# Values of the dilated attention stored from SBUF in three token orders, in place of copies from DRAM to DRAM

## The chip, the cores and the metric

The kernel runs on one core of a Trainium2 chip. The metric is the device time of one execution in microseconds (us); the median of three runs stands for a kernel. A core has five engines that run their own instruction streams in order: PE (matrix multiply), DVE (vector), ACT (scalar functions and copies), POOL, and SP, which here only issues DMAs. ACT issues DMAs too. Instructions wait for each other by semaphores.

## The reference

One decoder layer on 2048 tokens of width 1024, in float32: RMSNorm, one input projection, two attention mixers side by side, gates, and an output projection that is added to the input. Only the first mixer matters here. Its eight heads (64 wide) attend in three patterns at once, with strides 1, 4 and 16 between keys:

```
DILATED_PATTERNS = ((128, 1), (512, 4), (2048, 16))
proj = jnp.matmul(rmsnorm(x, norm_gain), w_in)
q_a, k_a, v_a, z_a, c_q, c_kv, k_rope, z_b = jnp.split(proj, idx, axis=-1)
v_a = v_a.reshape(B, S, A_HEADS, A_HEAD_DIM)
for window, dilation in DILATED_PATTERNS:
    o, m, den = dilated_pattern(q, k, v, rel_bias, window, dilation)
o_a = sum(alpha[..., None] * o)      # alpha: softmax over the three log denominators
mixed = concat([o_a * silu(z_a), o_b * silu(z_b)])
y = x + mixed @ w_out
```

In each pattern a token looks at the keys of its own residue class, so the values `v_a` are wanted by the kernel in three orders of tokens: as they are, grouped by residue modulo 4, and grouped by residue modulo 16.

## The kernel before

The first stage, up to some 705 us, is the input projection. It runs in two halves of eight token blocks (128 tokens each). In each half groups of columns follow each other: `g0 g1 q0 z0 q1 z1 k0 z2 k1 g2 z3` in half 0, `g0 g1 q0 q1 k0 k1 g2 z0 z1 z2 z3` in half 1 (lines 235 to 242). Per block, `mm_tok` (line 393) does 24 matmuls into one of three PSUM tiles, split in a high and a low part of both operands. The z groups (gates) multiply the other way round (`unit_z`, line 537) and keep their result in the DRAM tensors `GD`, through a tile `zst` of two buffers.

The values are in three of these groups: 64 columns in g0, 128 in g1, 320 in g2. `v_hi` (line 402) has ACT copy them from PSUM to the tile `vst`, which has two buffers; `v_lo` (line 407) stores them in the DRAM tensor `vA`, rows in the kernel's own order: within a block of 128 tokens the row is (residue modulo 16, then the eight tokens of that residue). `store` (line 180) puts a DMA off by one clock of the unit loop, `flush` (line 183) issues it from ACT. So there are 48 stores, one for each block and group.

`v_turn(n)` (line 411) then makes the other two orders for a quarter of the tokens, each by one copy of 1 MB from DRAM to DRAM issued from SP: `vA2` (order of stride 4, line 415) and `vA3` (order of stride 16, line 417). Quarters 0 and 1 are turned in the group q0 of half 1 (line 755), quarters 2 and 3 after the first loads of head 0 (lines 1265, 1266). These are places in the source: the first stage is not ordered by hand, a planner places the instructions on each engine's queue by its own estimates, and in the profile the copies stand at 310, 332, 567 and 588 us. From the second stage on, the order is written out by hand.

SP's queue in the first stage also carries the loads of the weights (`w_load`, line 246, into `wraw`, two buffers, freed by the splits of `w_split` on ACT, or POOL, and DVE, lines 271 to 274), of the input (`x_load`, line 194, three buffers `xt`), rows of the position bias (line 384) and, at its end, bias, Q and K of head 0 (`a_loadb`, `a_loadq`, `a_loadk`, lines 834, 814, 818). `h0`, `h1`, `h2` (lines 201 to 226) normalise a block of the input, transpose it on PE and split it into `hTh` and `hTl`.

The values are read in the second stage: `a_loadv(h, w)` (line 848) loads one head's columns of `vA`, `vA2` or `vA3`.

Of the kernel before, what the change touches and what calls it, by code (L numbers as in the profile page):

```python
# [101 lines left out]
def hybrid_kernel(ctx: ExitStack, tc: tile.TileContext, x, positions, rel_bias, norm_gain, w_in,  # L102
# [3 lines left out]
    pe, dve, act, pool, sp = nc.tensor, nc.vector, nc.scalar, nc.gpsimd, nc.sync  # L106
# [19 lines left out]
    vA = dr.tile([S, 512], F32, name="vA")  # L126
    vA2 = dr.tile([S, 512], F32, name="vA2")
    vA3 = dr.tile([S, 512], F32, name="vA3")
# [48 lines left out]
    deferred = []  # L177
    ends = []

    def store(dst, src):  # L180
        deferred.append((clock[0] + 1, dst, src))

    def flush(always=False):
        while deferred and (always or deferred[0][0] <= clock[0]):
            _, dst, src = deferred.pop(0)
            act.dma_start(dst, src)

    clock = [0]

# [4 lines left out]
    def x_load(b):  # L194
        XT[b] = xtile([128, D])
        sp.dma_start(XT[b], xv[b])
# [4 lines left out]
    def h0(b):  # L201
        st = P1.tile([128, 4], F32, name="hst", bufs=3)
        for u in range(2):
            act.activation(junk_tile(), XT[b][:, 512 * u:512 * u + 512], AF.Square, accum_out=st[:, 2 * u:2 * u + 1])
        dve.tensor_tensor(st[:, 1:2], st[:, 0:1], st[:, 2:3], op=OP.add)
        dve.tensor_scalar(st[:, 1:2], st[:, 1:2], 1.0 / D, EPS, op0=OP.mult, op1=OP.add)
        rstd_pow(st[:, 2:3], st[:, 1:2], 1)
        RST[b] = st
# [90 lines left out]
    for i, ap in enumerate((a_q_gain, a_k_gain, qn_gain, kn_gain)):  # L299
        src = bass.AP(tensor=ap.tensor, offset=ap.offset, ap=[[1, 64], [1, 1]])  # L300
# [104 lines left out]
        return v  # L405

    def v_lo(v, b, h0_):
        n = v.shape[1]
        store(vA[128 * b:128 * b + 128, 64 * h0_:64 * (h0_ + n)], v.rearrange("p h d -> p (h d)"))

    def v_turn(n):

        a, a2, a3 = vA[:], vA2[:], vA3[:]
        o = 512 * 512 * n
        sp.dma_start(bass.AP(tensor=a2.tensor, offset=a2.offset + o, ap=[[65536, 4], [4096, 16], [1, 4096]]),
                     bass.AP(tensor=a.tensor, offset=a.offset + o, ap=[[4096, 4], [16384, 16], [1, 4096]]))
        sp.dma_start(bass.AP(tensor=a3.tensor, offset=a3.offset + 16384 * n, ap=[[65536, 16], [4096, 4], [1, 4096]]),
                     bass.AP(tensor=a.tensor, offset=a.offset + o, ap=[[4096, 16], [65536, 4], [1, 4096]]))

    def qraw_tile():  # L420
        return P1.tile([128, 256], F32, name="qraw", bufs=5)
# [1 line left out]
    def unit_g0(key, b):  # L423
        st = {}

        def s1():
            ps = PS[key, b]
            m = st["m"] = P1.tile([128, 4], F32, name="cst", bufs=3)
            raw = st["raw"] = qraw_tile()
            act.activation(raw, ps[:, :256], AF.Copy)  # L430
            st["v"] = v_hi(1, ps[:, 256:320])
            act.activation(junk_tile()[:, :256], raw, AF.Square, accum_out=m[:, 0:1])

        def s2():
            m = st["m"]
            v_lo(st["v"], b, 0)
            dve.tensor_scalar(m[:, 1:2], m[:, 0:1], 1.0 / 256, EPS, op0=OP.mult, op1=OP.add)
            rstd_pow(m[:, 2:3], m[:, 1:2], 1)

        def s3():  # L440
            dve.tensor_scalar(st["raw"], st["raw"], st["m"][:, 2:3], None, op0=OP.mult)

        def s4():
            tp = tp_tile()
            for i in range(2):
                pe.transpose(tp[:, i, :], st["raw"][:, i * 128:(i + 1) * 128], ident)
            act.activation(cT[:, b % 8, 0:2, :], tp[:, 0:2, :], AF.Copy)

        return [lambda: mm_tok(key, 320, b), s1, s2, s3, s4]
# [39 lines left out]
    def unit_g2(key, b):  # L489
        st = {}  # L490

        def s1():
            st["v"] = v_hi(5, PS[key, b][:, :320])

        return [lambda: mm_tok(key, 320, b), s1, lambda: v_lo(st["v"], b, 3)]
# [41 lines left out]
    def unit_z(key, j, c, row):  # L537
        st = {}

        def s0():  # L540
            ps = st["ps"] = mm_tile() if P1 is not None else psZ.tile([128, 512], F32, name="mz", bufs=2)
            for k in range(8):
                mm3(ps, WH[key][:, k, j * 128:(j + 1) * 128], WL[key][:, k, j * 128:(j + 1) * 128],
                    hTh[c][:, k, :], hTl[c][:, k, :], k == 0, k == 7)

        def s1():
            t = PZ.tile([128, 512], F32, name="zst", bufs=ZST)
            act.activation(t, st["ps"], AF.Tanh, scale=0.5)
            dve.scalar_tensor_tensor(t, t, 1.0, st["ps"], op0=OP.add, op1=OP.mult)
            store(GD[row][:, c * 512:(c + 1) * 512], t)  # L550

        return [s0, s1]
# [128 lines left out]
    for gi, (half, nm) in enumerate(seq):  # L681
        key = (half, nm)
        units = []
        if nm[0] == "z":
            zi = int(nm[1])
            for c in (2 * half, 2 * half + 1):
                for j in range(2):
                    units.append(unit_z(key, j, c, 2 * zi + j))
        else:
            for b in range(8 * half, 8 * half + 8):  # L690
                if nm == "g0":
                    units.append(unit_g0(key, b))
                elif nm == "g1":
                    units.append(unit_g1(key, b))
                elif nm == "g2":
                    units.append(unit_g2(key, b))
                else:
                    units.append(unit_qk(key, b, 2 * int(nm[1]), nm[0] == "q"))
        nu = len(units)
        for i, unit in enumerate(units):  # L700
            if half == 1 and nm[0] == "z" and not (todo_bg or bg.live):
                late.append((gi, i, nu, unit))
                continue
            if nm == "g0" and half == 0:
                if i + 3 < 8:
                    x_load(i + 3)
                if i + 2 < 8:
                    h0(i + 2)
            if nm == "g0" and half == 1:
                b = 12 + i  # L710
                if i < 1:
                    x_load(b + 3)
                if i < 2:
                    h0(b + 2)
                if i < 4:
                    h1(b)
                    h2(b)
            clock[0] += 1
            flush()
            main.add(unit)  # L720
            main.tick()
            if nm == "g0" and half == 0 and i + 1 < 8:
                h1(i + 1)
                h2(i + 1)
            for u in (SPLIT8 if nu == 8 else SPLIT4)[i]:
                w_split(4 * gi + 4 + u)
            if half == 0 and gi == 9 and i == 5:
                for b in range(8, 11):
                    x_load(b)
            if half == 0 and gi == 9 and i in (6, 7):  # L730
                h0(2 + i)
            if half == 0 and gi == 10:
                if i == 0:
                    h0(10)
                    h1(8)
                if i == 1:
                    h1(9)
                if i == 2:
                    h2(8)
                    x_load(11)  # L740
                    h2(9)
                    x_load(12)
                    h1(10)
                    h0(11)
                if i == 3:
                    h2(10)
                    x_load(13)
                    h1(11)
                    h2(11)
                    x_load(14)  # L750
                    h0(12)
                    h0(13)
            if nm == "g0" and half == 0 and i == 5:
                rope_tables()
            if nm == "q0" and half == 1 and i in (0, 4):
                v_turn(i // 4)
            if nm == "g1":
                b = 8 * half + i
                todo_bg += [("q", b, clock[0]), ("k", b, clock[0] + 4)]
            credit = min(credit + RATE[half] * (1.5 if nm[0] == "z" else 1.0), 1.5)  # L760
            if credit >= 1 and todo_bg and todo_bg[0][2] <= clock[0]:
                credit -= 1
                kind, b, _ = todo_bg.pop(0)
                bg.add(post(b, kind))
            bg.tick()
            while ends:
                ends.pop(0)()
            if misc and not (nm == "g0" and half == 0):
                misc.pop(0)()
    main.drain()  # L770
    assert not ends
    while todo_bg:
        kind, b, _ = todo_bg.pop(0)
# [488 lines left out]
    a_loadq(0)  # L1262
    a_loadk(0, 0)
    a_loadk(0, 1)
    v_turn(2)
    v_turn(3)
    weave(zsteps[:ZC], seq_s(0))
    a_loadq(1)
    a_loadk(1, 0)
# [395 lines left out]
    for b in range(4, 16):  # L1665
        c, o = divmod(b, 4)
# [67 lines left out]
```

## Time and profile before

| | |
|---|---|
| median of three runs | 1694.55 us (1688.96 to 1695.15) |
| the profiled execution | 1694.15 us, span 1692.4 us |
| mean granted clock of TensorE in it | 0.983 |
| busy: PE, DVE, ACT, POOL | 1610.5, 963.2, 833.1, 670.7 us |
| DMA | 206.94 MB; read from HBM 139.60 MB, written 72.25 MB |

A profile is one execution. Its views name an instruction by line, engine, operation and tile; "idle before <-releaser" is the time in which its engine stood still before it, and what ended that. A wait in SP's or ACT's queue (SPq, ACTq) is that of the instruction that issues a DMA: it holds everything behind it on that engine. The granted clock is a share of 2.4 GHz.

### The profile page before, as it was taken

The numbers are of one execution on the slowest core, as the hardware profiler recorded it, in microseconds if no ns is written. First come the engines' busy times: TensorE is split into PE (matmuls) and PEld (weight loads), VectorE is DVE, ScalarE is ACT, GpSimd is POOL, SyncE is SP. The second block draws the span as 40 slices with busy tenths as digits, with TensorE's granted clock in tenths as the row PEclk, the third lists the DMA queues.
The fourth block names the chain that finished last, engine by engine and source line by source line (L and its number), as shares of the span: only waits on it lengthen the run. The fifth ranks groups of instructions, "written<-read, shape, count | busy, mean of one in ns | idle before, by whom it ended". The sixth has DMA issues, their size and how long they took to land. (4 is left out here: it accounts for less than half of the span.)

```text
span 1692.4 us, 29007 instructions
## 1 busy us (share of the span) xinstructions
PE 1610.5 (95%) x10028; PEld 1303.2 (77%) x10028; DVE 963.2 (57%) x2937; ACT 833.1 (49%) x2237; POOL 670.7 (40%) x699
## 2 busy tenths in 40 slices
PE   6999999989999979999999889999999999999998
PEld 5998899979999967888777566666666666567887
DVE  4655564254667215477778567767666666734331
ACT  5656454255666312458777755555555555530000
POOL 2364353014667101125565737754464361411000
PEclk8999999999999989999999999999999999999999
DMA  7357454551554683479985554312221221237652
GB/s 160 93 144 179 130 143 119 180 153 48 132 143 139 197 222 116 107 168 202 199 190 123 125 129 88 95 49 59 72 57 49 71 58 38 72 80 188 175 135 64
DMA packets 224711, 206.94 MB, mean 122 GB/s; under 512 B 102797, under 2 KB 189561, under 8 KB 218420
## 3 DMA queue, kind: packets, MB, share of 16 engines
q1 hardware_dynamic: 136852, 153.85, 36.3%
q10 hardware_dynamic: 87712, 51.24, 11.0%
q8 instruction: 79, 1.29, 0.3%
q14 instruction: 68, 0.56, 0.1%
HBM read 139.60 MB, written 72.25 MB: 125 GB/s over the span
## 5 line engine op out<-in xcount | busy, mean ns | idle before, releaser
L231 PE MATMUL mz<-wh,hTh 128*128 128x256 f32 (+2 forms) x600 | 182.9, 305 | 1.6 <-ACT hTh L225 1.6
L233 PE MATMUL mz<-wh,hTl 128*128 128x256 f32 (+2 forms) x600 | 179.0, 298 | 1.8 <-DVE hTl L226 1.8
L232 PE MATMUL mz<-wl,hTh 128*128 128x256 f32 (+2 forms) x600 | 178.1, 297 | 0.0
L1418 ACT ACTIVATE ptB<-T 128x512 f32<-128x512 f32 (+3 forms) x160 | 84.7, 529 | 169.2 <-PE T L1413 168.7
L1431 PE MATMUL O<-ptB,VB 128*64 128x512 f32 (+3 forms) x640 | 160.6, 559 | 2.0 <-DVE ptB L1416 2.0
L274 DVE SCALAR_TENSOR_TENSOR wl<-wraw,ng,wh 128x256 fp32r<-128x256 f32 (+2 forms) x176 | 83.1, 510 | 115.9 <-ACT wh L273 114.4
L1406 ACT ACTIVATE P<-P,msB 128x1024 f32<-128x1024 f32 (+4 forms) x104 | 109.4, 1052 | 65.5 <-DVE msB L1393 65.4
L1388 PE MATMUL S<-kBh,qBh 96*128 96x512 f32 (+2 forms) x320 | 133.4, 417 | 2.0 <-DVE msB L1393 2.0
L1388 PEld LDWEIGHTS S<-kBh,qBh 96*128 96x128 f32 x320 | 60.3, 189 | 94.0 <-issue 74.6
L231 PEld LDWEIGHTS mz<-wh,hTh 128*128 128x128 f32 x600 | 115.8, 193 | 3.8 <-ACT hTh L225 2.6
L233 PEld LDWEIGHTS mz<-wh,hTl 128*128 128x128 f32 x600 | 115.7, 193 | 2.6 <-DVE hTl L226 2.6
L1390 PE MATMUL S<-kBh,qBl 96*128 96x512 f32 (+2 forms) x320 | 116.7, 365 | 0.0
L1389 PE MATMUL S<-kBl,qBh 96*128 96x512 f32 (+2 forms) x320 | 116.5, 364 | 0.0
L232 PEld LDWEIGHTS mz<-wl,hTh 128*128 128x128 f32 x600 | 116.1, 193 | 0.1
L147 POOL TENSOR_TENSOR pst<-pst,CM 128x8 f32<-128x8 f32 x48 | 80.3, 1686 | 82.6 <-DVE pst L598 73.8
L273 ACT ACTIVATE wh<-wraw,ng 128x256 fp32r<-128x256 f32 (+2 forms) x168 | 76.5, 514 | 68.3 <-DMA wraw<-in_w_in_dram 40.2
L231 PE MATMUL po<-woh,mh 128*128 128x512 f32 x256 | 101.8, 398 | 2.7 <-ACT woh L1294 2.1
L1416 DVE COPY ptB<-T 128x512 f32<-128x512 f32 (+3 forms) x160 | 96.8, 605 | 12.3 <-PE T L1413 11.5
L1393 DVE CUSTOM_DVE_ANT_0 P<-S,zero 128x512 f32<-128x512 f32 (+1 forms) x96 | 65.1, 678 | 66.9 <-PE S L1390 65.2
L1413 PE MATMUL T<-CM,P 128*128 128x128 f32 x740 | 100.0, 276 | 2.5 <-DVE gA__12590 L1242 1.2
L232 PE MATMUL po<-wol,mh 128*128 128x512 f32 x256 | 100.4, 393 | 1.2 <-POOL wol L1295 1.2
L233 PE MATMUL po<-woh,ml 128*128 128x512 f32 x256 | 100.7, 394 | 0.0
(492 smaller groups left out, 4553.3 us busy)
## 6 DMA issues: line engine op xcount, KB each, us to landing
wraw<-in_w_in_dram SPq DMA_DIRECT2D x72, 256.0 KB
V<-vA SPq DMA_DIRECT2D x24, 512.0 KB
xt<-in_x_dram SPq DMA_DIRECT2D x16, 512.0 KB
GD<-zst ACTq DMA_DIRECT2D x32, 256.0 KB
vA<-vA SPq DMA_DIRECT2D x8, 1024.0 KB
Q<-qT SPq DMA_DIRECT2D x8, 1024.0 KB
KH<-kT SPq DMA_DIRECT2D x16, 512.0 KB
KL<-kT SPq DMA_DIRECT2D x16, 512.0 KB
```

Of the source, the lines that this page charges most:

```text
L231: pe.matmul(ps, lh, rh, start=first, stop=False)
L232: pe.matmul(ps, lh, rl, start=False, stop=False)
L233: pe.matmul(ps, ll, rh, start=False, stop=last)
L274: dve.scalar_tensor_tensor(WL[key][:, k, :w], r[:, j, :w], ng[:, k:k + 1], f32(wh), op0=OP.mult, op1=OP.subtract)
L1388: pe.matmul(ps[:, :nm], H["q", "h"][:, q], H["k", "h"][:, k], start=True, stop=False)
L1389: pe.matmul(ps[:, :nm], H["q", "h"][:, q], H["k", "l"][:, k], start=False, stop=False)
L1390: pe.matmul(ps[:, :nm], H["q", "l"][:, q], H["k", "h"][:, k], start=False, stop=True)
L1406: act.activation(t, t, AF.Exp, bias=b, scale=-1.0, accum_out=H["den", c][:, i, d:d + 1])
L1413: pe.transpose(tp[:, d, :], p_part(h, c, d, 128 * j, 128), ident)
L1416: dve.tensor_copy(pt[:, d0:, :], tp[:, d0:, :])
L1418: act.activation(pt[:, d0:, :], tp[:, d0:, :], AF.Copy)
L1431: pe.matmul(o[64 * e:64 * e + 64, d0:, :], V[:, j + e, :], pt[:, d0:, :], start=(j == 0), stop=(j == 4 * c + 2), skip_group_check=True)
```

## The change

`v_turn` and its eight copies are gone. `v_lo` stores each unit's values three times from `vst`: to `vA` from ACT as before, to `vA3` by one DMA from SP, and to `vA2` by four DMAs from SP, one for each 32 partitions, since the order of stride 4 splits a block into four places. `store` takes the issuing engine as an argument. So each of the 48 units has six DMAs in place of one (240 more, all on SP), of 128 rows or four times 32 rows of 256, 512 or 1280 bytes, and `vst` is free again when all six have landed.

```diff
-    def store(dst, src):
-        deferred.append((clock[0] + 1, dst, src))
+    def store(dst, src, eng=act):
+        deferred.append((clock[0] + 1, dst, src, eng))
 
     def flush(always=False):
         while deferred and (always or deferred[0][0] <= clock[0]):
-            _, dst, src = deferred.pop(0)
-            act.dma_start(dst, src)
+            _, dst, src, eng = deferred.pop(0)
+            eng.dma_start(dst, src)
...
     def v_lo(v, b, h0_):
+
         n = v.shape[1]
-        store(vA[128 * b:128 * b + 128, 64 * h0_:64 * (h0_ + n)], v.rearrange("p h d -> p (h d)"))
-
-    def v_turn(n):
-
-        a, a2, a3 = vA[:], vA2[:], vA3[:]
-        o = 512 * 512 * n
-        sp.dma_start(bass.AP(tensor=a2.tensor, offset=a2.offset + o, ap=[[65536, 4], [4096, 16], [1, 4096]]),
-                     bass.AP(tensor=a.tensor, offset=a.offset + o, ap=[[4096, 4], [16384, 16], [1, 4096]]))
-        sp.dma_start(bass.AP(tensor=a3.tensor, offset=a3.offset + 16384 * n, ap=[[65536, 16], [4096, 4], [1, 4096]]),
-                     bass.AP(tensor=a.tensor, offset=a.offset + o, ap=[[4096, 16], [65536, 4], [1, 4096]]))
+        cols = slice(64 * h0_, 64 * (h0_ + n))
+        v = v.rearrange("p h d -> p (h d)")
+        store(vA[128 * b:128 * b + 128, cols], v)
+        store(vA3[:].rearrange("(i m a) c -> m i a c", i=16, a=8)[b, :, :, cols], v, sp)
+        for x in range(4):
+            store(vA2[:].rearrange("(n j x a) c -> n x j a c", n=4, j=4, a=8)[b // 4, 4 * (b % 4) + x, :, :, cols],
+                  v[32 * x:32 * x + 32], sp)
...
-            if nm == "q0" and half == 1 and i in (0, 4):
-                v_turn(i // 4)
...
-    v_turn(2)
-    v_turn(3)
```

## Rows read from the trace of the kernel before

**Rows 1.** First part of the page: busy time and share of the span.

```profile
PE 1610.5 (95%) x10028; PEld 1303.2 (77%) x10028; DVE 963.2 (57%) x2937; ACT 833.1 (49%) x2237; POOL 670.7 (40%) x699
```

**Rows 2.** Busy time by stretch; columns: us, PE, PEld, DVE, ACT, POOL, clock, DMA, GB/s.

```profile
66.00:98.00 32.00, 32.00 (x222) 28.53 (x221) 16.98 (x57) 20.68 (x83) 19.55 (x44) 1.00 0.38 110
...
296.00:324.00 28.00, 28.00 (x188) 27.54 (x187) 3.38 (x8) 5.48 (x14) 1.00 (x1) 1.00 0.61 190
...
344.00:362.00 18.00, 11.04 (x58) 10.17 (x57) 7.93 (x17) 9.47 (x25) 1.02 (x2) 0.82 0.64 183
580.00:645.00 65.00, 50.37 (x214) 40.69 (x212) 16.83 (x59) 13.26 (x29) 3.90 (x7) 0.89 0.71 198
```

**Rows 3.** Timeline of PE, 340 to 362 and 580 to 645: instructions after a gap.

```profile
348.20 0.84 PE L222 MATMUL tp<-CM,xt 128*128 128x128 f32 x4 [3.65 <-DVE hTl L226]
359.44 1.09 PE L222 MATMUL tp<-CM,xt 128*128 128x128 f32 x4 [3.31 <-DVE hTl L226]
...
582.22 0.33 PE L634 MATMUL tp<-CM,krr 128*128 128x128 f32 x1 [1.77 <-ACT sg L641]
603.31 0.79 PE L231 MATMUL mz<-hTh,wh 128*128 128x512 f32 x1 [4.40 <-DVE zst L549]
...
617.33 0.59 PE L891 MATMUL S<-KH,Q 128*128 128x256 f32 x3 [2.96 <-DMA KH<-kT]
...
638.70 0.58 PE L891 MATMUL S<-KH,Q 128*128 128x256 f32 x1 [4.85 <-DVE m L903]
```

**Rows 4.** Stretches just after these gaps, same columns as rows 2.

```profile
348.00:350.00 2.00, 1.79 (x9) 1.61 (x10) 1.34 (x3) 0.30 (x1) 0.00 (x0) 0.64 0.90 243
350.00:352.00 2.00, 2.00 (x10) 2.00 (x9) 0.00 (x0) 0.00 (x0) 0.00 (x0) 0.51 0.71 206
...
360.00:362.00 2.00, 2.00 (x10) 1.96 (x9) 1.36 (x4) 1.71 (x7) 0.46 (x1) 0.50 0.92 278
...
603.00:606.00 3.00, 2.69 (x6) 2.15 (x7) 1.05 (x3) 0.91 (x2) 0.00 (x0) 0.50 0.49 154
606.00:609.00 3.00, 3.00 (x11) 2.38 (x10) 0.77 (x2) 0.60 (x1) 1.20 (x2) 0.67 0.91 339
618.00:621.00 3.00, 3.00 (x9) 2.37 (x8) 0.00 (x0) 0.00 (x0) 0.00 (x0) 0.53 1.05 201
...
639.00:642.00 3.00, 3.00 (x14) 2.84 (x14) 3.00 (x12) 0.00 (x0) 0.00 (x0) 0.50 0.37 92
```

**Rows 5.** Waits of SP's queue, 300 to 375 and 560 to 690: total us, times, longest.

```profile
SPq L196 <- DMA vA<-vA: 8.9, 1, 8.9
...
SPq L837 <- DMA vA<-vA: 11.6, 1, 11.6
```

**Rows 6.** Timeline of ACT, 304 to 372 and 562 to 700: the long waits.

```profile
346.23 0.60 ACT L548 ACTIVATE zst<-mz 128x512 f32<-128x512 f32 x1 [9.69 <-DMA GD<-zst]
...
581.15 0.44 ACT L404 ACTIVATE vst<-mz 128x320 f32<-128x320 f32 x1 [8.36 <-DMA vA<-vst]
...
601.94 0.60 ACT L548 ACTIVATE zst<-mz 128x512 f32<-128x512 f32 x1 [10.73 <-DMA vA<-vA]
```

**Rows 7.** A stretch with a copy in flight, same columns as rows 2.

```profile
345.00:347.00 2.00, 0.00 (x0) 0.00 (x0) 0.14 (x1) 0.77 (x2) 0.00 (x0) 1.00 0.24 102
```

**Rows 8.** Timeline of ACT, 30 to 35: a value store and the copy that waits.

```profile
31.24 0.35 ACTq L186 DMA_DIRECT2D vA<-vst  x1
...
34.34 0.22 ACT L404 ACTIVATE vst<-mm 128x64 f32<-128x64 f32 x1 [0.48 <-DMA vA<-vst]
```

**Rows 9.** Issue of DMAs: ns min/median/max by tile, and one series on SP's timeline.

```profile
L186 ACTq DMA_DIRECT2D vA<-vst x48: 326/326/482, 31.2 to 585.8; - x48
...
L196 SPq DMA_DIRECT2D xt<-in_x_dram x16: 536/556/1440, 0.7 to 367.1; - x16
...
87.13 5.67 SPq L384 DMA_DIRECT2D biasD<-BV  x8
```

**Rows 10.** Third part of the page: HBM traffic.

```profile
HBM read 139.60 MB, written 72.25 MB: 125 GB/s over the span
```

## The prediction

> **What bounds the kernel now.** I read the page's first part: PE is busy for 95% of the span [rows 1]. So only a change that shortens PE's gaps, or makes new ones, moves the end. Then I read the stretches in which the change acts: the projection stage, up to about 705 us. In its value groups PE has no gap in the half-0 stretches (66 to 98 and 296 to 324 us), but from 344 to 362 it loses 6.96 of 18 us and from 580 to 645 it loses 14.63 of 65 [rows 2]. Both stretches follow a pair of copies. What lies behind (about 990 us of attention and output projection) reads the same tensors from the same places and is taken as unchanged: what the first 700 us gain or lose, the end gains or loses.
>
> PE's own timeline says what ended each gap: 3.65 and 3.31 us in the first stretch, 1.77, 4.40, 2.96 and 4.85 in the second [rows 3]. After the longer gaps the granted clock stands near 0.5, that is 1.2 GHz instead of 2.4: busy time times the missing share of the clock is 0.64 + 0.98 + 1.00 = 2.6 us in the first stretch and 1.35 + 0.99 + 1.41 + 1.50 = 5.3 us in the second [rows 4]. So at most 6.96 + 2.6 + 14.63 + 5.3 = 29.5 us are to be had here.
>
> **What leads from the copies to these gaps.** SP's waits show issues that stood behind a copy though they read nothing of it: an x load for 8.9 us, head 0's bias load (with Q and K behind it) for 11.6 us [rows 5]. ACT shows the same: it waited 9.69 us for a GD store before the gate unit at 346.23, 8.36 us for a vA store before 581.15, 10.73 us for a copy before 601.94 [rows 6]. And in 345 to 347, when little but a copy is in flight, the DMA engines are 0.24 busy and move 102 GB/s [rows 7]: about a quarter of them work, so a copy of 1 MB has a tail of some 10 us (1 MB by 102 GB/s).
>
> **Removed: the eight copies.** (a) Turn of the halves. The gap of 3.65 us stands behind ACT's 9.69 us for the GD store. An undisturbed vA store frees its tile 3.1 us after issue (31.24 to 34.34, [rows 8]); by that the wait shrinks by some 6.6 us, more than the gap. Gain 3.65 + 1.6 of clock = 5.3. The gap of 3.31 us follows the late x load. Without the copy's 8.9 us the load starts earlier than PE's 5.3, but it must still wait for its tile; I take 3 of 3.31 + 1.0. Sum (a) 8.3. (b) End of the stage. 1.77 and 4.40 hang on ACT's 8.36 and 10.73: with their clock (1.35 + 0.99) 8.5. The gap of 2.96 us (K of head 0) and 1.41 of clock go as well, since the loads come up to 11.6 us earlier and PE only 8.5. What is late next is the gap of 4.85 us: it waits for reductions that stand on DVE behind weight splits, fed by weight loads that share the DMA engines with Q and K. That chain moves with the loads, by 11.6, so I cap (b) at 11.6. Together **-19.9**; low end -13.8 (only 5.3 + 8.5), high end -29.5.
>
> **Added: 240 DMAs on SP.** Each of 48 units now has one vA store on ACT as before, and one vA3 and four vA2 stores on SP. The trace does not show these forms. The nearest are the x loads (the same regrouped pattern of tokens): 0.556 us each at issue; the bias rows, eight in 5.67 us or 0.71 each with gaps; below stands the flat vA store with 0.326 [rows 9]. I take 0.7, the row that has a series of them: 3.5 us of SP for each unit, 168 us over six value groups (bounds 78 and 170). A unit of g2 lasts 28/8 = 3.5 us and one of g1 32/8 = 4 us [rows 2], so SP is just kept busy there, and the weight loads, x loads and bias rows queue behind stores that themselves wait for ACT's copy out of PSUM.
>
> The tile of values (vst) has two buffers, and ACT's next-but-one copy waits for all six DMAs: 0.4 (the copy) + 4 x 0.7 (issues before the last) + 3.1 = 6.3 us, against two units, 7 to 8 us. So in steady state it fits by under a microsecond. Behind a waiting ACT stand the copies out of PSUM, the splits of weights and all stores of q, k and gates; PE waits for them only when its three PSUM tiles are full, two units or 7 us later. That cover is there in g1 and g2. It is not at the start: units 0 and 1 are copied out within half a microsecond, and unit 2's copy at 34.34 would wait until 31.2 + 2.8 + 3.1 = 37.1, some 3 us, with the halves of h that PE needs behind it. I take 3 for that, 1.5 for g1 of half 0 (SP also carries bias rows there) and 1.5 for g0 of half 1 (x loads behind the stores): **+6**, between 0 (all covered) and 19 (3.1 in each of the six groups). Traffic: the stores write what the copies wrote and read SBUF, so 8.4 of the 139.6 MB read from HBM go [rows 10]; nothing in PE's time hangs on that share.
>
> The projection stage is not ordered by hand: a planner places each queue's instructions by its own estimates. All queues there may shift by some microseconds either way; that is in the range, not in the sum.
>
> The Trainium skill speaks against the change: "DMA: Bandwidth & Descriptors", section Bandwidth, calls transfers under 64 KB descriptor-dominated (0.68 us for 4 KB, 0.95 for 64 KB) and wants 1 MiB each. By these figures, as an estimate, the 240 stores would be 160 to 230 us of DMA work, against eight copies at 6.15 us; no run here shows such stores in number, and the sum goes by the rows above.
>
> **Sum.** 1694.15 (the profiled execution, span 1692.4) - 19.9 + 6 = **1680**; that execution stands 0.4 us under the median of 1694.55.
>
> **The rivals.**
> 1. Slower: small stores that free their tile late. If the last of the six lands L us after its issue, ACT's cycle for two units is 3.2 + L instead of 7.0, and a value group of eight units loses 4 x (L - 3.8) less the cover of 7: 4L - 22. Six groups give 24L - 133. That equals the gain of 19.9 at L = 6.4, the point from which it decides; at L = 7 it is +35, and the time 1694 - 20 + 35 = 1709. For it: a quarter store has the outer count of 4 that the vA2 copy has, so it may use a quarter of the DMA engines like that copy [rows 7]; and a store beside a copy held ACT for 8.36 us [rows 6]. Against it: 3.1 us for an undisturbed store, and at 102 GB/s on a quarter of the engines four stores of 40 KB need 1.6 us of the 3.5. The Trainium skill, "DMA: Bandwidth & Descriptors" (Why a DMA increments its semaphore by 16 and not by 1), has the count of engines divide the outermost counts of both sides, which would be 4 for the quarter stores; by that rule this mechanism is there and its price stays the 1.6 us just given, and the copy's row agrees with it.
> 2. No difference: the gaps move and don't close. PE meets the weight loads or Q and K a few microseconds later instead of the copies. With (a) 5.3, (b) 4.4 and the cost of 6 the time is 1690. For it: in 603 to 645 the DMA engines are busy with head loads whatever came before, and the last gap is not a copy's. Against it: the named waits of 8.9, 10.73 and 11.6 us end at copies alone.
> 3. All gaps close and the stores are covered: 1694 - 27 = 1667. Against it: the last gap.
> 4. The planner puts the stores where they do nothing for the copies' place (for instance the V loads wait for them): then the two stretches keep their gaps. I see nothing for it; it is in rival 2.
>
> **How the numbers follow.** Forecast with rival 3, 0.57; rival 2, 0.21; rival 1, 0.22. A measurement of this kernel can tell about 0.5%, 8.5 us, from no change: faster is under 1686, slower over 1703. The range runs from 1667 (rival 3) to 1704, which leaves out the worse half of rival 1 and little else.
>
> **What would show it.** Right: no instruction waits for a copy; PE's stretch around 344 to 362 has at most one gap of under 2 us; head 0's loads start some 10 us earlier; HBM reads near 131 MB; ACT's waits for vst stay under 3 us each. Wrong: ACT waits for vst by 4 us and more in every value group, PE gaps in g1 or g2, weight loads late behind SP's stores, or head 0's loads no earlier than before.

## The result and the profile after

| | before | after |
|---|---|---|
| median of the runs on one chip | 1691.97 us (4 runs) | 1671.86 us (4 runs, 1668.79 to 1672.27) |
| the profiled execution, its span | 1694.15, 1692.4 us | 1672.27, 1670.5 us |

The ratio is 0.9877, 95% interval [0.9855, 0.9898]: about 20 us faster (21.9 between the two profiled executions). The forecast was 1680 in a range of 1667 to 1704.

From the page of the changed kernel, its first and third part (against [rows 1, 10]):

```profile
PE 1608.2 (96%) x10028; PEld 1300.6 (78%) x10028; DVE 965.4 (58%) x2937; ACT 834.3 (50%) x2237; POOL 670.5 (40%) x699
...
q1 hardware_dynamic: 150084, 153.86, 37.1%
q10 hardware_dynamic: 87712, 51.24, 11.2%
...
HBM read 131.21 MB, written 72.25 MB: 122 GB/s over the span
```

PE does the same matmuls in a shorter span; the 8.4 MB that the copies read are gone. The time is found in the two stretches that the prediction named. Busy time by stretch before (columns as in [rows 2]):

```profile
336.00:386.00 50.00, 43.04 (x273) 40.85 (x272) 23.75 (x57) 26.11 (x76) 6.68 (x11) 0.93 0.50 145
575.00:660.00 85.00, 70.37 (x331) 58.83 (x330) 25.93 (x101) 17.87 (x39) 6.65 (x11) 0.92 0.60 170
```

And after:

```profile
336.00:386.00 50.00, 47.16 (x310) 43.67 (x310) 25.57 (x63) 29.53 (x88) 7.53 (x12) 1.00 0.53 124
575.00:660.00 85.00, 83.18 (x411) 70.02 (x410) 35.25 (x140) 19.09 (x44) 12.44 (x22) 1.00 0.69 190
```

Busy time times granted clock rises from 40.0 to 47.2 us and from 64.7 to 83.2: 25.7 us more of work in the same 135 us, of which the end keeps 21.9. PE's own timeline of the changed kernel in 335 to 395 and 560 to 680, every gap over 0.3 us:

```profile
348.88 0.63 PE L222 MATMUL tp<-CM,xt 128*128 128x128 f32 x4 [0.81 <-DVE xt L211]
366.26 1.37 PE L222 MATMUL tp<-CM,xt 128*128 128x128 f32 x8 [1.35 <-DVE xt L211]
369.72 0.63 PE L222 MATMUL tp<-CM,xt 128*128 128x128 f32 x4 [0.34 <-DVE cst L435]
...
616.91 0.50 PE L231 MATMUL mz<-hTh,wh 128*128 128x512 f32 x1 [1.04 <-DVE zst L547]
619.36 0.36 PE L887 MATMUL S<-KH,Q 128*128 128x256 f32 x1 [0.78 <-DVE m L899]
```

Of the six gaps in [rows 3], 20.9 us together, 1.82 us are left at the end of the stage and 2.50 at the turn of the halves. The last of them, 4.85 us behind the reductions `m` on DVE, is 0.78 us now. The granted clock is 1.00 in both stretches.

Two lines of SP's timeline, before and then after, show where the second stage's values are loaded, and so how much earlier the hand-ordered part starts:

```profile
684.41 0.37 SPq L852 DMA_DIRECT2D V<-vA  x1
```

```profile
660.57 20.76 SPq L848 DMA_DIRECT2D V<-vA  x3
```

23.8 us earlier; the work behind that load takes 1009.9 us in place of 1008.0.

The price of the change is seen on ACT and SP. ACT's waits for a buffer of `vst`, in 290 to 335 and in 540 to 590 us (total, times, longest), and SP's stores in the last value group, with SP's own waits among these 30 stores:

```profile
ACT vst L404 <- DMA vA<-vst: 12.7, 4, 4.5
...
ACT vst L404 <- DMA vA<-vst: 11.4, 4, 5.5
```

```profile
557.38 24.52 SPq L186 DMA_DIRECT2D vA<-vst  x30
...
583.78 0.46 SPq L833 DMA_DIRECT2D braw<-biasD  x1
```

```profile
SPq L186 <- DMA vA<-vst: 3.2, 2, 2.8
SPq L186 <- DMA wraw<-in_w_in_dram: 1.3, 2, 0.8
SPq L186 <- DMA kT<-qst__7519: 1.3, 2, 0.8
SPq L186 <- DMA kR<-sg: 0.2, 1, 0.2
```

These are all of ACT's waits for the value stores, 24.0 us: they lie in g2, none in g0 or g1. They are no longer than before, when ACT waited 25.7 us for its own stores, all but 2.5 of it after a copy had been issued; with the copies made small (first experiment) it waits 2.1. So the change puts waits for stores where the copies had put them. SP's 30 stores take 24.52 us, but 6.0 of these it waits, for an earlier store or another DMA; the rest is 0.62 us a store. Head 0's bias load comes right behind them (before: 603.93). In g0 of half 1 it is SP's queue that costs: an x load stands behind stores for which SP had waited 3.3 us, ACT waits for the load, and the PE gap of 1.35 us follows. SP's timeline and ACT's:

```profile
356.14 1.27 SPq L186 DMA_DIRECT2D vA<-vst  x2
357.52 0.58 SPq L196 DMA_DIRECT2D xt<-in_x_dram  x1
358.15 0.63 SPq L186 DMA_DIRECT2D vA<-vst  x1
358.89 0.56 SPq L196 DMA_DIRECT2D xt<-in_x_dram  x1
```

```profile
362.85 0.63 ACT L204 ACTIVATE junk<-xt 128x512 bf16<-128x512 f32 x1 [3.43 <-DMA xt<-in_x_dram]
```

### The profile page after: what moved, and what is told of

Read it like the earlier page. It is cut to its first block, busy times and chain, and to the rows that moved or that the text cites. A ratio compares the mean times of both kernels' runs of the same rounds, so it can differ in the third digit from the quotient of the medians.

```text
span 1670.5 us, 29350 instructions
## 1 busy us (share of the span) xinstructions
PE 1608.2 (96%) x10028; PEld 1300.6 (78%) x10028; DVE 965.4 (58%) x2937; ACT 834.3 (50%) x2237; POOL 670.5 (40%) x699
## 3 DMA queue, kind: packets, MB, share of 16 engines
q10 hardware_dynamic: 87712, 51.24, 11.2%
HBM read 131.21 MB, written 72.25 MB: 122 GB/s over the span
## 4 chain that ended last, share of the span: by engine, by line
PE 80%; DMA 9%; ACT 4%; DVE 3%; POOL 1%; issue 1%; SPq 1%; ACTq 0%; DVEq 0%; POOLq 0%
PE O L1425 9%; PE T L1407 7%; PE mz L233 7%; PE mz L231 7%; PE mz L232 7%; PE S L1382 5%; PE S L1384 4%; PE S L1383 4%; PE po L231 3%; PE po L233 3%; PE po L232 3%; PE mm L233 3%; PE mm L231 3%; PE mm L232 3%; PE S L887 3%; DMA rbA<-rD 2%
## 5 line engine op out<-in xcount | busy, mean ns | idle before, releaser
L147 POOL TENSOR_TENSOR pst<-pst,CM 128x8 f32<-128x8 f32 x48 | 80.1, 1680 | 76.6 <-DVE pst L596 70.2
L1410 DVE COPY ptB<-T 128x512 f32<-128x512 f32 (+3 forms) x160 | 96.7, 605 | 12.3 <-PE T L1407 11.6
```

Source lines behind the costliest of these rows:

```text
L1410: dve.tensor_copy(pt[:, d0:, :], tp[:, d0:, :])
```

## Experiments

Three theories of the gain and its price were to be told apart. T1: the copies themselves, with the waits that named them, cost what the gain shows, and the stores give some microseconds of it back. T2: it is the order of things in the queues (the planner orders the whole stage anew) that moved the end. T3, on the copies alone: a wide copy would have done as well, because only the narrow one has a long tail. Then two on the stores' price: the two-buffer cycle of `vst`, or SP's issuing.

**The copies made small.** On the kernel before:

```diff
-  ap=[[65536, 4], [4096, 16], [1, 4096]]   <-  ap=[[4096, 4], [16384, 16], [1, 4096]]
+  ap=[[65536, 4], [4096, 16], [1, 64]]     <-  ap=[[4096, 4], [16384, 16], [1, 64]]
   (the same for vA3)
-        va = (vA, vA2, vA3)[w - 1][:]
+        va = vA[:]
```

> The kernel before with each of the eight copies cut to a 64th of its bytes (256 bytes of each 16 KB run), in their old places in the queues; the attention of strides 4 and 16 reads its values from vA, so the values there are in another order. No new stores. Theory 'copies in the way': the copies' bytes are the whole gain, so this is 18 to 24 us faster than the kernel before, about 1670. Rival 'planner': the gain of the change comes mostly from the other order in which the planner places the projection stage; then this, which keeps that order up to 600 us, gains under 8 us, over 1684.

Measured: 1665.89 us (1664.11 to 1667.98), ratio 0.9837 [0.9816, 0.9858], 27.6 us faster than the kernel before. PE in this kernel, busy time by stretch and the gaps over 0.3 us of the second stretch:

```profile
336.00:386.00 50.00, 50.00 (x353) 48.63 (x352) 27.71 (x70) 33.50 (x104) 9.68 (x18) 1.00 0.44 106
575.00:660.00 85.00, 83.38 (x419) 70.20 (x418) 32.59 (x136) 27.76 (x86) 12.21 (x22) 1.00 0.65 177
```

```profile
591.73 0.35 PE L891 MATMUL S<-KL,Q 128*128 128x256 f32 x1 [0.57 <-DMA KL<-kT]
605.91 0.35 PE L891 MATMUL S<-KH,Q 128*128 128x256 f32 x1 [0.99 <-DVE m L903]
```

The gaps go, the 4.85 us one too. But the copies did not stay in their old places, as the expectation had it. A small copy reads only the 64 columns that g0 stores, and the planner puts each pair right behind g0, at 40, 67, 367 and 381 us, for instance:

```profile
366.75 0.68 SPq L415 DMA_DIRECT2D vA<-vA  x1
```

Before, they stood behind g2, at 310, 332, 567 and 588 us, and the first of each half held SP for 7.3 and 5.9 us until values had landed. So this run takes away the copies' bytes and their places in SP's queue together: 27.6 us is what the copies cost as they stood, and bytes and place are not told apart here. PE's order is that of before up to some 607 us, so the turn of the halves at least owes nothing to another order on PE. Against this run the changed kernel lacks 0.0040 of 1692, some 7 us (the two intervals just meet). I take that as the price of the stores; the order of instructions differs between the two as well, so it is a difference of two kernels and no measurement of the stores alone.

**Which of the two copies.** Only vA2's copies made small, then only vA3's, each with its own order read from `vA` instead. Again the small ones move up behind g0; the whole ones stay behind g2.

> The kernel before with the four vA2 copies (outer count 4) cut to a 64th of their bytes; the four vA3 copies (outer count 16) whole; the attention of stride 4 reads vA. Theory 'narrow tail': the vA2 copy was the larger part, 18 to 25 us faster than the kernel before, 1668 to 1675. Rival 'bytes': half the bytes, half the gain of 27.6: about 1680.

> The kernel before with the four vA3 copies cut to a 64th and the four narrow vA2 copies whole; the attention of stride 16 reads vA. Theory 'narrow tail': most of the loss stays, 4 to 10 us faster than the kernel before, 1683 to 1690. Rival 'bytes': half the gain of 27.6: about 1680 or less.

Measured: without vA2's bytes 1676.78 us, ratio 0.989 [0.9865, 0.9914], -18.6; without vA3's 1681.32, ratio 0.9934 [0.9914, 0.9954], -11.2. The sum, 29.8, is near the 27.6 of both. The narrow copy costs more (the two intervals just meet), but the wide one isn't free.

**The narrow copy made wide.** The same bytes to the same places, with the two outer dimensions swapped on both sides; the order of instructions on every engine, SP included, is that of the kernel before:

```diff
-  ap=[[65536, 4], [4096, 16], [1, 4096]]   <-  ap=[[4096, 4], [16384, 16], [1, 4096]]
+  ap=[[4096, 16], [65536, 4], [1, 4096]]   <-  ap=[[16384, 16], [4096, 4], [1, 4096]]
```

> The kernel before with the two outer dimensions of the vA2 copy swapped on both sides, so that the outer count is 16 and no longer 4: the same bytes and the same order of all instructions. Theory 'narrow tail': the vA2 copy runs on a quarter of the DMA engines for some 10 us and holds what shares them; with 16 the tail goes from the DMA share (no stretch at 0.24 with 100 GB/s) and half of the gain comes, 8 to 14 us faster, about 1681. Rival 'bytes': 8 MB read and 8 MB written are in the way however they are spread; within 4 us of the kernel before, 1688 to 1696.

Measured: 1676.11 us (1666.62 to 1678.93), ratio 0.9887 [0.986, 0.9914], -19. Stretches with a pair of copies in flight, before and then here, and the longest wait of an x load for a copy and the largest PE gap that is left:

```profile
311.00:317.00 6.00, 6.00 (x43) 6.00 (x42) 0.00 (x0) 0.88 (x2) 0.00 (x0) 1.00 0.72 209
```

```profile
311.00:317.00 6.00, 6.00 (x43) 6.00 (x42) 0.00 (x0) 0.78 (x2) 0.00 (x0) 1.00 1.00 349
```

```profile
SPq L196 <- DMA vA<-vA: 2.4, 1, 2.4
...
600.22 0.60 PE L891 MATMUL S<-KH,Q 128*128 128x256 f32 x3 [4.85 <-DMA KH<-kT]
```

The share of the DMA engines is 1.00 in place of 0.72, and the 8.9 us of [rows 5] are 2.4. The turn of the halves is then free of gaps; at the end of the stage K of head 0 still comes late beside the second pair of copies. T3 is right for nearly the whole of the net gain: swapping two dimensions gives what the 240 stores give. And since bytes, places and order are those of before, T2 has no part in these 19 us: this run shows the copies' hold on the queues (T1) by itself. It is more than the 8 to 14 us expected, and as much as without vA2's bytes (18.6): within the intervals, what the narrow copy costs is its form.

**One store and one wide copy.** vA3 by one SP store per unit, vA2 by the wide copies.

> Half of the change: vA3 by one store a unit from SP (48 in all), vA2 still by four copies of 1 MB, with the outer count 16 of the wide copy. Theory: SP is far from full with one store a unit (0.65 of 3.5 us), and only half of the copies' bytes are left, in the form that cost least: 1664 to 1672, as fast as the changed kernel or up to 8 us faster. Rival 'bytes next to the head loads': two copies still fall beside the loads of head 0 and hold them: 1674 to 1680.

Measured: 1673.89 us (1671.83 to 1678.51), ratio 0.9887 [0.9867, 0.9908]: as the changed kernel. ACT waits 2.2 us for stores, and K of head 0 is late again (PE gaps 1.81 and 1.93 us). One price is exchanged for the other; the time lies between the ranges of the theory and of its rival.

**Stores and copies together.** The changed kernel, with the eight copies kept as well, into tensors that nothing reads.

> The changed kernel with the eight copies put back in their old places, into two tensors that nobody reads. Theory 'copies in the way': it loses the gain, 15 to 25 us slower than the changed kernel, 1687 to 1697. Rival 'planner': it stays near the changed kernel, 1668 to 1680.

Measured: 1715.05 us (1712.17 to 1716.71), ratio 1.0126 [1.0104, 1.0148]: 43 us over the changed kernel, well above the expectation. PE's largest gaps:

```profile
378.49 0.63 PE L233 MATMUL mz<-wh,hTh 128*128 128x320 f32 x1 [6.92 <-ACT hTh L227]
...
631.31 0.98 PE L900 MATMUL S<-KH,Q 128*128 128x256 f32 x3 [7.18 <-DMA wraw<-in_w_in_dram]
```

The planner put the copies at 341 to 346 and at 603 and 621, right at the x loads and among head 0's loads (braw at 604.19). The same eight copies cost 27.6 us as they stood before and 43 here, where they lie elsewhere and beside the stores; which of the two makes the difference isn't told apart. T2 has this much right, that the planner's places matter.

**Twice the small stores.** Each quarter store issued a second time into a tensor that nothing reads: nine SP stores for a unit instead of five.

> The changed kernel with the four quarter stores of each unit issued twice, the second time into a tensor that nobody reads: nine stores of 0.65 us a unit on SP, 5.9 us against 3.5 to 4 us of PE. Theory 'just covered': five stores a unit fit under PE and nine don't; a value group of eight units loses 8 x (5.9 - 3.75) = 17 us less the 7 us that the PSUM tiles cover, six groups some 60 us: 1710 to 1735. Rival 'far from the bound': stores are hidden at twice their number too, 1670 to 1680.

Measured: 1742.33 us (1738.93 to 1749.17), ratio 1.0294 [1.0269, 1.032]: 70 us over the changed kernel. PE's waits that name a value copy, and ACT's for these stores:

```profile
PE mz L232 <- ACT vst L405: 23.1, 11, 8.3
PE mm L232 <- ACT vst L405: 6.4, 4, 2.8
...
ACT vst L405 <- DMA vX<-vst: 33.1, 9, 7.5
```

Rival 1 of the prediction is real: stores free the tile late, ACT waits, PSUM stays full, PE stops. At five stores it doesn't reach PE (no wait of PE names a value copy); at nine it costs more than the whole change gains. PE's two rows are 29.5 of the 70 us; the planner's order is another one too, and the rest was not followed.

**Is it SP's queue?** In g2, two of each unit's four quarter stores from ACT:

```diff
-                  v[32 * x:32 * x + 32], sp)
+                  v[32 * x:32 * x + 32], act if n == 5 and x > 1 else sp)
```

> The changed kernel with two of the four quarter stores of each g2 unit issued from ACT, which is busy for under a third of that group; g0 and g1 as they were. SP has three stores of 0.65 us a g2 unit and no longer five. Theory 'SP's queue is the cost': in the changed kernel the x loads and the loads of head 0 stand behind g2's stores; they come 5 to 7 us earlier here, and the time is 1664 to 1668. Rival 'DMA engines': the stores' bytes on few engines are the cost, whoever issues them: 1670 to 1675. Rival 'ACT': ACT's own issues delay its copies out of PSUM: over 1675.

Measured: 1680.45 us (1675.77 to 1681.85), ratio 0.9918 [0.99, 0.9937], some 7 us over the changed kernel. ACT waits 26.6 us for the stores, head 0's bias load starts at 584.16, and K is late:

```profile
604.30 0.98 PE L887 MATMUL S<-KH,Q 128*128 128x256 f32 x3 [5.67 <-DMA KH<-kT]
```

The theory of SP's queue alone falls: with 16 issues fewer on SP head 0's loads come no earlier (583.78 in the changed kernel). The time is in the range of the rival 'ACT', but the trace shows ACT waiting for stores to land and not held by its issues. PE's order differs from that of the changed kernel from g2 of half 0 on, so the 7 us are not all the stores'.

**Is it the two buffers?** Three buffers for `vst`. For room, `qraw` has four instead of five; the control has that alone. The control's PE order is that of the changed kernel, but with three buffers the planner orders every engine a little differently from some 34 to 64 us on, so, other than the two expectations say, the pair differs in order too.

> The changed kernel with three buffers for the tile of values (vst) instead of two; to make room in SBUF the tile qraw has four buffers instead of five, which shifts part of the order of the first stage (the run beside this one has that alone). Theory (the some 6 us that the stores cost lie in the cycle of the two vst buffers, because ACT's copy of unit n+2 waits for six stores of unit n): with a third buffer ACT's waits for vst, 24.0 us in the changed kernel, fall under 8; group g2 of half 1 lasts 28 to 29 us from its first to its last value copy (31.9 in the changed kernel, 28.4 without copies or stores); head 0's loads and the end come 3 to 6 us earlier than in the run beside it, about 1666 where the changed kernel has 1672. Rival (SP issues the five stores of a unit no faster than 3.75 us, so SP's queue sets the cycle whatever the number of buffers): g2 still lasts 31 us and more, the time is within 2 us of the run beside it.

> The control of the run before: the changed kernel with four buffers for qraw and two for vst, in the same order of instructions as the run with three. Both theories: within 3 us of the changed kernel, 1669 to 1676, ACT's waits for vst 20 to 28 us.

Measured: three buffers 1668.75 us (1664.51 to 1669.59), ratio 0.9842 [0.9825, 0.9859]; the control 1676.22 (1667.16 to 1679.55), ratio 0.9891 [0.9872, 0.991]. Value copies of the last g2 and the waits before them, with three buffers and then in the control:

```profile
L404 ACT ACTIVATE vst<-mz x6: 437/437/437, 544.3 to 572.7; 128x320 f32<-128x320 f32 x6
...
  PE mz L233: 12.5, 6
  DMA vA<-vst: 3.1, 1
```

```profile
L404 ACT ACTIVATE vst<-mz x6: 437/438/440, 544.4 to 576.2; 128x320 f32<-128x320 f32 x6
...
  DMA vA<-vst: 11.5, 5
  PE mz L233: 1.4, 2
```

With three buffers ACT waits for PE again, not for stores, and the group takes 28.4 us, as without copies. But SP, three and then two buffers:

```profile
569.71 12.03 SPq L186 DMA_DIRECT2D vA<-vst  x14
...
583.06 0.46 SPq L833 DMA_DIRECT2D braw<-biasD  x1
```

```profile
569.71 11.66 SPq L186 DMA_DIRECT2D vA<-vst  x15
...
582.42 0.46 SPq L833 DMA_DIRECT2D braw<-biasD  x1
```

The stores end at the same time and head 0's loads come no earlier. So the expectation holds for the group and for the repeated times (the two intervals lie apart by little), not for the loads; and ACT's waits for `vst` fall to 10.5 us in all, not under 8 (25.1 in the control). The two profiled executions, 1669.59 and 1667.16, don't show the gain (the control's is its fastest of five), so where it lies, and whether the buffer or the other order brings it, stays open. Against the changed kernel, 0.9842 to 0.9877, the intervals overlap at the edge: three buffers are probably better by a few microseconds.

**Three buffers and less on SP.**

> Three vst buffers (and four of qraw) as before, and in group g2 two of the four quarter stores of each unit from ACT, so that SP issues three stores a unit there (24 in place of 40 in g2 of half 1). Theory (two limits in a row: the vst cycle, lifted by the third buffer, and then SP's queue, in which head 0's loads stand behind the last stores; SP's stores ended at 581.7 us with two and with three buffers): g2 of half 1 lasts 28 to 29 us, SP's last store of it ends at 577 or earlier, head 0's loads start at 575 to 579 (583.1 with three buffers alone), and the time falls below the run with three buffers alone (1668.75), to 1663 to 1667. Rival (what stands in front of head 0's loads is not SP's issuing but the arrival of the last values or the weight loads): head 0's loads no earlier than 582, time 1668 to 1676, as when two of the four were moved with two buffers (1680).

Measured: 1674.67 us (1668.54 to 1678.3), ratio 0.9861 [0.9836, 0.9885]: no better than three buffers alone. SP's last value stores, and the loads behind them, with a wait:

```profile
570.48 3.76 SPq L186 DMA_DIRECT2D vA<-vst  x4
576.85 0.35 SPq L833 DMA_DIRECT2D braw<-biasD  x1
582.53 0.34 SPq L834 DMA_DIRECT2D bias<-biasD  x1
...
SPq L834 <- DMA vA<-vst: 4.7, 1, 4.7
```

The first load comes 6.2 us earlier, as the theory said; the second then waits for a value store to land, and Q starts at 583.04 (584.72 with three buffers alone). So the rival holds here: not SP's issuing but the arrival of the last values is in front of head 0's loads. What limits that arrival wasn't found; SP's waits between stores in the changed kernel (6.0 us, shown with the result) were not followed to their cause.

## Why the prediction was right, and where it was not

The forecast was 8 us too slow: faster than before by 14, measured 20. Its mechanism is the one that acted; the gain at the end of the stage was too small, and the stores' price came out at the right size for partly wrong reasons.

**Right.** Copies hold issues that read nothing of them: with the vA2 copy made wide, in an unchanged order, the x load's wait for a copy falls from 8.9 to 2.4 us and the gaps at the turn close. Term (a), the turn of the halves, was 8.3. With small copies the first value copy of g0 in half 1 comes 10.3 us earlier (361.19 before, 350.87), 1.4 of which were won before the turn. A quarter of the engines for the vA2 copy [rows 7] fits the swap of dimensions. The Trainium skill, "DMA: Bandwidth & Descriptors" (Why a DMA increments its semaphore by 16 and not by 1), has the count of engines divide the outermost counts of both sides, which is 4 for this copy and 16 after the swap. The DMA shares of 0.72 and 1.00 agree with it.

**The step that failed: the cap of 11.6 on the end of the stage.** It took SP's 11.6 us wait before head 0's loads [rows 5] as all that the copies held there, and let the chain of the 4.85 us gap move with it. But the copies had delayed more than that: from the first value copy of the last g2 (551.62) to the loads (603.93) it took 52.3 us, and with small copies it takes 31.4 (540.02 to 571.43), 20.9 less. 4.7 of these lie in the group, which lasts 33.2 us before, with ACT's 8.36 [rows 6] in it, and 28.4 with small copies. The other 16.2 lie behind it on SP, between the weight load at 586.55 and head 0's loads: 11.6 are the wait that the cap took, the rest is two copies and one more weight load that are issued there, with their own waits. A weight load waited for a copy too:

```profile
SPq L253 <- DMA vA<-vA: 12.9, 1, 12.9
```

This row of before was in the same view as that of [rows 5] and was not read. It doesn't simply add to the 11.6: the load that waited 12.9 us here waits for a weight split when the copies are small (16.6 us), and starts only 4.7 us earlier after the group's first copy. So neither the last wait nor the sum of the waits is the gain; the distance between two points of the chain is. From the first value copy of that g2 to the V load it is 132.8 us before, 115.2 after and 110.2 with small copies: 17.6 and 22.6 won, in place of the 11.6. And the gap of 4.85 us, which was to move, closed to 0.78, and to 0.99 with small copies. The sum with all gaps closed (29.5, put down as the high end) is near what the copies really cost, 27.6.

**Stores: right size, partly the wrong place.** The +6 is some 7 measured, and that the two agree is chance. Of its terms one is borne out: 1.5 for g0 of half 1, x loads behind the stores, is the PE gap of 1.35 us at 366. The 3 at the start and the 1.5 in g1 of half 0 are not there: ACT waits for no store in either; at the start the planner ordered unit 2's copy at 39.69 us, behind a weight load. What was left out lies in g2, where the prediction saw a fit "by under a microsecond" and where all 24.0 us of ACT's waits are. The issue was not sized too small: 0.62 us each without waits, 3.1 for a unit, where 0.7 was taken and PE needs 3.5 [rows 2]. Left out was that SP, in order, stands still between the stores of one unit. The third unit's five stores in the last g2:

```profile
557.38 5.16 SPq L186 DMA_DIRECT2D vA<-vst  x5
```

They take 5.16 us in place of 3.1, ACT's longest wait, 5.5 us, ends when they have landed, and the fourth unit's stores stand behind them. The cover that was named, PSUM, holds, so PE has no gap there, but the group's last values come late, and head 0's loads with them: 38.4 us after the group's first value copy (545.39 to 583.78), against 31.4 with small copies. Between the changed kernel and that one, the profiled executions put 2.1 us before g2 of half 0 (299.34 and 297.28, not followed to a wait), 3.3 from there to g2 of half 1 and 5.0 from there to the V load (115.2 against 110.2); 2.5 of the sum come back behind it.

**Rivals.** 1: not at five stores, and real at nine. Its point of decision, 6.4 us from issue to landing, was not reached: in the last g2 ACT's copies start 3.0 to 4.6 us after the issue of the last store that they wait for. The DMA engines' time hardly rises: the two large queues take 47.3% of 1692.4 us before and 48.3% of 1670.5 after, 800.5 and 806.9 us of all sixteen; with small copies it is 46.7% of 1662.6, 776.4, so the stores add some 30 us and the copies had taken 24. The estimate by the Trainium skill's figures ("DMA: Bandwidth & Descriptors", Bandwidth), 160 to 230 us of DMA work for the stores, is not borne out by these 30 us. The Trainium skill gives these figures for loads from HBM issued by GpSimd, so this run says nothing against the figures themselves. 2: fell, since the last gap closed. 3: came nearest in gaps, but with the stores' price, which it took as covered. 4: fell.

**What would show it.** No instruction waits for a copy (there is none), HBM reads are 131.21 MB and the 344 to 362 stretch has one gap of 0.81 us (and one of 0.20): as said. Head 0's loads were to come 10 us earlier and come 20.2. ACT's waits under 3 us: wrong, up to 5.5.

## What to carry to other kernels

Where long transfers hold several issues, follow the chain through all of them, not the last wait alone; the chance of "all gaps close" is then larger than it looks. A named wait is not yet a gain, since another can stand in its place (12.9 us named, 4.7 won). Before a copy from DRAM to DRAM is rebuilt, look at the DMA share while it runs and at its outermost count: here a swap of two dimensions gave nearly as much as the rebuilding. Stores in many small pieces are paid on the issuing queue and in the buffer that they empty, so count pieces per unit against the unit's time: five (3.1 us of issues for 3.5 us of PE) left PE without a gap, nine did not. Where a planner places the instructions, a copy that is made smaller may depend on less and move: here it did.

## What the runs showed of the hardware

- An issue of a store takes SP 0.58 us in the median (the flat one on ACT 0.33); with the short pause between two it is 0.62 in the row of 30, SP's waits taken off. Issues on SP (ns, min/median/max):

```profile
L186 SPq DMA_DIRECT2D vA<-vst x240: 554/582/1212, 31.0 to 581.3; - x120
```

- With a pair of DRAM to DRAM copies of 1 MB in flight the kernel moved 209 or 349 GB/s, at a DMA share of 0.72 or 1.00, by the order of one copy's outer dimensions alone.
